# One weight pool for a whole encoder program, with reordered block products and convolution taps that are spread over the next unit

## The chip, the cores and the metric

The kernel runs on one core of a Trainium2 chip. The metric is the time of one execution on the device, in microseconds (us). The engines are PE (TensorE: matrix products), DVE (VectorE), ACT (ScalarE), POOL (GpSimd) and SP (SyncE), whose queue issues nearly all DMAs here. PE accumulates into PSUM banks, which the other engines read; everything else lies in SBUF, 128 partitions wide.

## The reference

One step of a four-part encoder trunk with model width D = 1024 on T = 1152 columns (1024 tokens of a prompt and 8 x 16 tokens of samples). Every part is normalised ahead and added to the stream x:

```
x += attention(rms_norm(x)) @ w_attn_out      # w_attn_in: 1024 -> 3072; 8 band heads, 4 differential heads
x += (silu(h @ wg) * (h @ wu)) @ wd           # h = rms_norm(x), width 2816, twice in all
gb, gc, u = split(rms_norm(x) @ w_conv_in, 3) # 1024 -> 3072
x += (gb * conv3(gc * u)) @ w_conv_out        # three taps along the tokens, one weight per channel
x += (silu(h @ wg) * (h @ wu)) @ wd
y = rms_norm(x)
```

The attention also returns keys and values, the convolution its last two inputs. All of it is float32.

## The kernel before

x lies transposed, as eight tiles of 128 channels by T columns. A float32 product is made of three: each operand is split into a high part, which ACT casts, and a low part, the rest, which DVE subtracts, and PE adds high x high, low x high and high x low (`mm3`, L164 to L166; `pairs`, L1170 to L1172; `unit`, L1033 to L1035).

**Weights.** A piece of 128x512 float32 (256 KB) is loaded by `raw` (tile r, L858) and split by `part` into h (ACT, L868) and l (DVE, L869); RAWS = 5 raw and PARTS = 5 split pieces are in flight. These belong to the pool "w2", which is opened when the attention has closed its own pool. The attention's blocks use another pool, "w1", through `weights`: pieces of 128x1024 (512 KB; tiles wr, wh, wl; L152 to L156), two of each.

**Stages.** The first norm and the attention take up to 645 us of the profiled execution. While the attention's heads are worked off on ACT, DVE and POOL, PE is kept busy with blocks of the in- and out-projection. The last heads' columns of the out-projection (weights in_w_aol) are done by `pairs`, which also serves the three wide products down, conv-out and down: j over 4 pairs of output tiles, six accumulations of 384 columns each; with j = 0 the first inputs k < nk - 1 (here three of four) of all six are done ahead of the last one. Then follow the gates of the first FFN (717 to 1205 us), its down product, the convolution's in-product (1486 to 1796 us), its out-product, and the second FFN, whose down product `down_last` ends the program together with the final norm.

**Units.** Gates and the convolution's in-product are done in units by a seven-product scheme in place of eight (Winograd's form of Strassen's algorithm). A unit has products n = 0 to 6, each in two column halves s of 12 matmuls of 128x288. ORDER names for each the left operand (a sum of weight quarters, made by DVE additions, L990), the right operand (sums of activations, tb11h, tt3h and so on) and the PSUM zone. Behind each half `self.tick()` counts down the pieces of work in `self.late`, so there are 14 ticks in a unit. With product a11, ACT copies the zone to u (L1048) and DVE adds zone b into g (L1049); later DVE adds follow (L1052 to L1065, L1022), POOL multiplies by the norm's factor rb (L1062). With a11 third, the next product, a12, goes into the zone that a11's copy reads.

**The convolution.** A group j has three units: two make the gated inputs xi of channel tiles f, the third the output gate. When a unit of the first kind ends, `end` writes xi and makes the three taps at once: POOL the last one (L1133), DVE the two others (L1136, L1137), POOL the product with rb (L1138).

**The first norm.** Each tile x is split into hh (ACT for even m, POOL for odd m, L196, L198) and hl (DVE, L199); squares on ACT (L207), their sums on POOL for m <= 2, else on DVE (L215); then PE column sums, the root on DVE, diagonals on ACT and POOL (L275, L277), and a spread by PE (L285).

**The order.** A scheduler places the instructions of each engine by priority. Each engine and the SP queue then run their own list in order, and wait where an operand or a buffer isn't ready.

Of the kernel before, what the change touches and what calls it, by code (L numbers as in the profile page):

```python
# [19 lines left out]
P = 128  # L20
D = 1024
# [15 lines left out]
NY = 11  # L37
# [5 lines left out]
NT = 17  # L43
# [56 lines left out]
class K:  # L100
# [45 lines left out]
    def weights(self, src):  # L146

        nc = self.nc
        self.n += 1
        n = self.n  # L150
        raw = self.wp.tile([P, 8, P], F32, tag="wr", name=f"wr_{n}", bufs=2)
        nc.sync.dma_start(raw, src)  # L152
        hi = self.wp.tile([P, 8, P], F32R, tag="wh", name=f"wh_{n}", bufs=self.wbufs)
        lo = self.wp.tile([P, 8, P], F32R, tag="wl", name=f"wl_{n}", bufs=self.wbufs)
        nc.scalar.copy(hi, raw)
        nc.vector.tensor_tensor(lo, raw, hi.bitcast(F32), ALU.subtract)  # L156
        return hi, lo
# [21 lines left out]
    def product(self, ps, w, h, c, step=None):  # L179
        self.mm3(ps, [(w[0][:, k, :], w[1][:, k, :], h[k][0][:, c], h[k][1][:, c]) for k in range(KT)], step)  # L180


    def begin_norm(self, gi, htile, pp, tag, tmp=None, early=False):
        return {"gi": gi, "h": [None] * KT, "rb": [None] * NB, "acc": [None] * NB, "new": htile, "pp": pp, "tag": tag, "tmp": tmp or self.small, "early": early}

    def norm_tile(self, st, m, b, xb):
# [3 lines left out]
        if st["new"] is not None:  # L190
            if st["h"][m] is None:
                st["h"][m] = (st["new"]("hh"), st["new"]("hl"))
            hi, lo = st["h"][m]
            gs = self.g[:, st["gi"], m:m + 1]
            if st["early"] and m % 2:
                nc.gpsimd.tensor_scalar(hi[:, c], xb, gs, 1.0, ALU.mult, ALU.mult)  # L196
            else:
                nc.scalar.activation(hi[:, c], xb, AF.Copy, scale=gs)  # L198
            nc.vector.scalar_tensor_tensor(lo[:, c], xb, gs, hi[:, c].bitcast(F32), ALU.mult, ALU.subtract)  # L199
# [3 lines left out]
    def norm_sum(self, st, m, b, xb):  # L203
        nc = self.nc
        tp = st["tmp"]
# [6 lines left out]
        else:  # L212
            acc = tp("ssq")
            eng = nc.vector if (st["early"] and m > 2) or (st["new"] is None and (m % 2 or m > 5)) else nc.gpsimd
            eng.tensor_tensor(acc, st["acc"][b], sq, ALU.add)  # L215
# [12 lines left out]
    def norm_end(self, st, b):  # L228

        tp = st["tmp"]  # L230
        ps = self.sums(st["pp"], st["tag"], st["acc"][b])
        r = self.rstd(ps[:, :3], D, *[self.tmp(t, (P, 3)) for t in "vty"])
# [11 lines left out]
    def sums(self, pp, tag, sq):  # L244

        ps = self.psum(pp, tag)
        for j in range(3):
# [15 lines left out]
    def diagonals(self, r, tp):  # L263

        nc = self.nc
        parts = self.tmp("rp", (P, 2, 3), F32R)
# [3 lines left out]
        for p in range(2):  # L270
            dg = tp("diag", F32R)
            for j in range(3):
# [8 lines left out]
    def spread(self, pp, tag, dg):  # L281

        ps = self.psum(pp, tag)
# [5 lines left out]
    def accumulate(self, pp, x, y, wsrc, step=None, banks="g"):  # L289
# [4 lines left out]
        for mg in range(KT // per):  # L294
            w = self.weights(wsrc[mg])
            for m in range(mg * per, (mg + 1) * per):
                for b in range(NB):
                    mm = m % per
                    ps = self.psum(pp, banks[(m * NB + b) % len(banks)], (P, 512))[:, :BLK]
                    self.mm3(ps, [(w[0][:, mm * nk + k, :], w[1][:, mm * nk + k, :], y[k][0][:, cut[b]], y[k][1][:, cut[b]]) for k in range(nk)], step)  # L300
# [392 lines left out]
    def subln(self, pp, h):  # L693

        nc = self.nc
        for b in range(NB):
# [7 lines left out]
            r = self.rstd(ps[:, :3], 2 * HD, *[self.tmp(t, (P, 3)) for t in "vty"])  # L704
# [6 lines left out]
    def attention(self, c):  # L711
# [11 lines left out]
        self.wp = pool(right, "w1", side="right")  # L723
        self.wbufs = 2
# [10 lines left out]
        st = self.begin_norm(0, new, pp, "t", self.early, early=True)  # L735
# [107 lines left out]
    def small(self, name, dt=F32):  # L843

        n = {"sq": 4, "ssq": 4, "rb": 3, "diag": 2}[name]
        at = {"sq": 0, "ssq": 4, "rb": 8, "diag": 12}[name] + self.turn.get(name, 0) % n
        self.turn[name] = self.turn.get(name, 0) + 1
        t = self.bits[at // 3][:, at % 3 * BLK:(at % 3 + 1) * BLK]
# [132 lines left out]
    ORDER = (("s2", "t2", "b"), ("s1", "t1", "c"), ("a11", "b11", "a"), ("a12", "b21", "a"), ("s3", "t3", "b"), ("a22", "t4", "b"), ("s4", "b22", "c"))  # L981

    def left_sides(self, w1, w2):
# [12 lines left out]
        split = {"s1": self.part(s1)}  # L996
        s2 = add(s3, a22)
        split["s2"] = self.part(s2)
        split["a11"] = self.part(a11)
# [9 lines left out]
    def unit(self, pp, st, weights, by, end, last=False):  # L1009
# [26 lines left out]

        if first:
            for n in range(3):
                for s in range(2):
                    products(n, s, range(2 if n == 2 else 3))  # L1040
        for n, (wn, p, zn) in enumerate(order):
            for s in range(2):
                products(n, s, range(4) if not first or n > 2 else range(2 if n == 2 else 3, 4))
                ps = zone[zn, s]
                self.tick()
                if n == 2:
# [25 lines left out]
            if n + PARTS < len(order):  # L1072
                ahead = order[n + PARTS][0]
# [29 lines left out]
    def conv(self, pp, st):  # L1103
# [4 lines left out]
        for j in range(KT // 2):  # L1108
            cv = {}
            for f in (2 * j, 2 * j + 1):  # L1110
# [7 lines left out]
                def end(s, g, u, xp=xp, xs=xs, f=f, cv=cv):  # L1118
# [14 lines left out]
                    nc.gpsimd.tensor_scalar(v[:, :SEQ], xp[:, 2:], tap[2], 1.0, ALU.mult, ALU.mult)  # L1133
                    nc.gpsimd.tensor_scalar(vs, xs[:, :, 2:], tap[2], 1.0, ALU.mult, ALU.mult)
                    for t in (1, 0):
                        nc.vector.scalar_tensor_tensor(v[:, :SEQ], xp[:, t:t + SEQ], tap[t], v[:, :SEQ], ALU.mult, ALU.add)  # L1136
                        nc.vector.scalar_tensor_tensor(vs, xs[:, :, t:t + DS], tap[t], vs, ALU.mult, ALU.add)  # L1137
                    nc.gpsimd.tensor_tensor(v, v, st["rb"], ALU.mult)  # L1138
                    cv[f] = v
# [87 lines left out]
    def down_last(self, pp, x, wsrc, chunks):  # L1227
# [14 lines left out]
        self.bits = [self.take("bits")[0] for _ in range(5)]  # L1242
        self.turn = {}
        st = self.begin_norm(4, None, pp, "n")

        def final(b, q, rb):
            for m in (5, 0, 6, 1, 7, 2, 3, 4):
                xb = x[m][:, b * BLK:(b + 1) * BLK]
                if m > 4:
# [3 lines left out]
                nc.sync.dma_start(o["yT"][m][:, b * BLK:(b + 1) * BLK], xb)  # L1253

        st["then"] = final
        for b in range(NB):
            c = slice(b * BLK, (b + 1) * BLK)
            for m in range(KT):
                ps = self.psum(pp, "g", (P, 512))[:, :BLK]
# [4 lines left out]
    def run(self):  # L1264
# [4 lines left out]
        self.xd = self.dp.tile([KT, P, T], F32, name="xd")  # L1269
        x, y = self.attention(c)  # L1270
        with ExitStack() as c:
            pool = lambda name, **kw: c.enter_context(tc.tile_pool(name=name, bufs=1, side="right", reuse_waits="tile", **kw))
            self.wp = pool("w2")
# [133 lines left out]
```

## Time and profile before

| | |
|---|---|
| time, median of 3 runs | 2694.86 us (2690.82 to 2698.37) |
| the profiled execution's own time | 2701.08 us |
| its span, first to last instruction | 2699.2 us |
| mean granted TensorE clock in it | 0.983 |
| PE busy | 2609.2 us, 97% |
| DVE, ACT, POOL busy | 64%, 35%, 22% |
| down, 1250 to 1500 us | PE busy all the time, clock 1.00 |

PE is the engine that sets the time, so its idle time and the stretches with a lower clock are what can be gained without changing the products. The clock column of the profile gives the mean over the stretch; the two levels behind it are 2.4 GHz (1.00) and 1.2 GHz (0.50).

### The profile page before, as it was taken

To read this page: it belongs to the slowest core of one execution; us is meant where nothing else is said; L and a number is where in the kernel's file an instruction comes from. 1 tells how busy PE (TensorE), PEld (TensorE's weight loads), DVE (VectorE), ACT (ScalarE), POOL (GpSimd) and SP (SyncE) were. 2 spreads that over 40 slices of the span, in tenths; PEclk is the share of its full clock that TensorE was granted. 3 is DMA by queue.
4 is the path that set the end of the run, shared out by engine and by line. 5 is a ranking of instruction groups with operands and counts; after the bars stand their busy time and mean duration, and the time that the engine had idled before them with its cause. 6 is when DMAs were issued, how large, how long until landed. Compare 5 with 4: busy or idle time off the path is not lost. (4 is left out here: it accounts for less than half of the span.)

```text
span 2699.2 us, 45160 instructions
## 1 busy us (share of the span) xinstructions
PE 2609.2 (97%) x17440; PEld 2568.3 (95%) x17440; DVE 1715.0 (64%) x3498; ACT 935.1 (35%) x1761; POOL 581.2 (22%) x651
## 2 busy tenths in 40 slices
PE   7999999998999999999999999999999999999997
PEld 6899999988999999999999999999999999999997
DVE  7667766676966666665327877776766666673325
ACT  5555444453532222232104322224422222231114
POOL 6434233320022222220000322320122222210002
PEclk9999999999999999999999999999999999999999
DMA  5654565561022222244212122252322222262211
GB/s 193 186 172 153 169 186 175 173 213 59 32 89 78 77 75 74 76 130 147 69 44 89 49 79 75 62 178 81 117 93 74 74 77 77 76 207 81 66 40 71
DMA packets 179542, 285.71 MB, mean 106 GB/s; under 512 B 38528, under 2 KB 108032, under 8 KB 179328
## 3 DMA queue, kind: packets, MB, share of 16 engines
q1 hardware_dynamic: 179328, 282.84, 33.4%
q8 instruction: 137, 2.24, 0.3%
q14 instruction: 77, 0.63, 0.1%
HBM read 206.67 MB, written 76.10 MB: 105 GB/s over the span
## 5 line engine op out<-in xcount | busy, mean ns | idle before, releaser
L868 ACT CAST h<-r 128x512 fp32r<-128x512 f32 x496 | 305.8, 618 | 960.1 <-PE ps_g L1034 421.6
L869 DVE TENSOR_TENSOR l<-r,h 128x512 fp32r<-128x512 f32 x496 | 359.2, 726 | 127.0 <-ACT h L868 111.8
L1170 PE MATMUL ps_g<-yh,h 128*128 128x384 f32 x1152 | 387.6, 336 | 0.0
L1172 PE MATMUL ps_g<-yh,l 128*128 128x384 f32 x1152 | 387.5, 336 | 0.0
L1171 PE MATMUL ps_g<-yl,h 128*128 128x384 f32 x1152 | 386.7, 336 | 0.0
L1062 POOL TENSOR_TENSOR u<-u,rb 128x576 f32<-128x576 f32 x98 | 158.2, 1634 | 743.2 <-DVE u L1022 725.9
L1183 DVE TENSOR_TENSOR x<-ps_g,x 128x384 f32<-128x384 f32 x240 | 129.4, 552 | 235.3 <-PE ps_g L1172 234.8
L1170 PEld LDWEIGHTS ps_g<-yh,h 128*128 128x128 f32 x1152 | 216.7, 188 | 0.4 <-DVE x L1183 0.2
L1171 PEld LDWEIGHTS ps_g<-yl,h 128*128 128x128 f32 x1152 | 216.5, 188 | 0.0
L1172 PEld LDWEIGHTS ps_g<-yh,l 128*128 128x128 f32 x1152 | 216.4, 188 | 0.0
L164 PE MATMUL ps_g<-hh,wh 128*128 128x384 f32 x544 | 194.4, 358 | 8.9 <-ACT hh L198 6.8
L165 PE MATMUL ps_g<-hl,wh 128*128 128x384 f32 x544 | 186.8, 343 | 1.5 <-DVE hl L199 1.4
L166 PE MATMUL ps_g<-hh,wl 128*128 128x384 f32 x544 | 186.1, 342 | 0.8 <-DVE wl L156 0.8
L990 DVE TENSOR_TENSOR r<-r,r 128x512 f32<-128x512 f32 x224 | 170.8, 762 | 24.8 <-DMA r<-in_w_gu 12.5
L1097 DVE TENSOR_TENSOR g<-g,u 128x576 f32<-128x576 f32 x88 | 66.5, 758 | 148.7 <-ACT g L1096 148.7
L1033 PE MATMUL ps_g<-tb21h,h 128*128 128x288 f32 x448 | 137.4, 307 | 22.2 <-ACT u L1048 22.2
L1033 PE MATMUL ps_g<-tt4h,h 128*128 128x288 f32 x448 | 134.5, 300 | 7.6 <-DVE u L1057 7.6
L1033 PE MATMUL ps_g<-tt3h,h 128*128 128x288 f32 x448 | 135.1, 302 | 2.3 <-DVE g L1049 2.3
L1033 PE MATMUL ps_g<-tb22h,h 128*128 128x288 f32 x448 | 132.9, 297 | 4.5 <-DVE u L1022 4.5
L1035 PE MATMUL ps_g<-tb21h,l 128*128 128x288 f32 x448 | 136.4, 305 | 0.0
L1034 PE MATMUL ps_g<-tb21l,h 128*128 128x288 f32 x448 | 136.1, 304 | 0.0
L1034 PE MATMUL ps_g<-tt3l,h 128*128 128x288 f32 x448 | 134.2, 300 | 0.0
(274 smaller groups left out, 7379.7 us busy)
## 6 DMA issues: line engine op xcount, KB each, us to landing
r<-in_w_gu SPq DMA_DIRECT2D x176, 256.0 KB, 2.7
y<-yd SPq DMA_DIRECT2D x52, 576.0 KB, 4.7
yd<-g SPq DMA_DIRECT2D x96, 288.0 KB, 2.5
r<-in_w_down SPq DMA_DIRECT2D x88, 256.0 KB, 2.7
wr<-in_w_in SPq DMA_DIRECT2D x24, 512.0 KB, 4.4
r<-in_w_cin SPq DMA_DIRECT2D x48, 256.0 KB, 2.7
xd<-x SPq DMA_DIRECT2D x16, 576.0 KB, 2.8
x<-xd SPq DMA_DIRECT2D x16, 576.0 KB, 5.6
```

The source lines that it names most:

```text
L164: nc.tensor.matmul(ps, wh, xh, start=(j == 0), stop=False)
L165: nc.tensor.matmul(ps, wh, xl, start=False, stop=False)
L166: nc.tensor.matmul(ps, wl, xh, start=False, stop=(j == n - 1))
L868: self.nc.scalar.copy(hi, raw)
L869: self.nc.vector.tensor_tensor(lo, raw, hi.bitcast(F32), ALU.subtract)
L990: nc.vector.tensor_tensor(t, x_, y, ALU.add)
L1033: nc.tensor.matmul(ps, w[0][:, k, :], hi, start=(new and k == 0), stop=False, skip_group_check=True)
L1034: nc.tensor.matmul(ps, w[0][:, k, :], lo, start=False, stop=False, skip_group_check=True)
L1062: nc.gpsimd.tensor_tensor(zu[s], zu[s], self.cols(by()[1], s), ALU.mult)
L1170: nc.tensor.matmul(ps, w[q][0][:, e, :], ys[k][0][0][:, c], start=(k == 0), stop=False, skip_group_check=True)
L1171: nc.tensor.matmul(ps, w[q][0][:, e, :], ys[k][1][0][:, c], start=False, stop=False, skip_group_check=True)
L1172: nc.tensor.matmul(ps, w[q][1][:, e, :], ys[k][0][0][:, c], start=False, stop=(k == nk - 1), skip_group_check=True)
```

## The change

- One pool "w" is opened ahead of the attention and stays to the end. `weights` now takes two pieces of 128x512 from it by `raw` and `part`, so the attention shares the five raw and five split pieces with all that follows.
- ORDER has a11 second and s1 third; the pieces are split in that order. The first unit behind a norm keeps the products' old order (seq = 0, 2, 1, 3, ...).
- The taps are entered in `late` and come 1, 2, 4 and 6 ticks into the next unit. The product with rb is DVE's now.
- In the first norm all hh are ACT's and all sums of squares DVE's, as in the last norm.
- `down_last` cuts the columns at 512 and 896, so the last block has 256 columns; the sharing of the final products between POOL and DVE follows the blocks.
- Two buffer counts differ by one (NY, NT).

```diff
-NY = 11
+NY = 10
...
     def weights(self, src):
 
-        nc = self.nc
-        self.n += 1
-        n = self.n
-        raw = self.wp.tile([P, 8, P], F32, tag="wr", name=f"wr_{n}", bufs=2)
-        nc.sync.dma_start(raw, src)
-        hi = self.wp.tile([P, 8, P], F32R, tag="wh", name=f"wh_{n}", bufs=self.wbufs)
-        lo = self.wp.tile([P, 8, P], F32R, tag="wl", name=f"wl_{n}", bufs=self.wbufs)
-        nc.scalar.copy(hi, raw)
-        nc.vector.tensor_tensor(lo, raw, hi.bitcast(F32), ALU.subtract)
-        return hi, lo
+        parts = [self.part(self.raw(src[:, 4 * q:4 * q + 4, :])) for q in range(2)]
+        return [(hi[:, k, :], lo[:, k, :]) for hi, lo in parts for k in range(4)]
...
-            if st["early"] and m % 2:
-                nc.gpsimd.tensor_scalar(hi[:, c], xb, gs, 1.0, ALU.mult, ALU.mult)
-            else:
-                nc.scalar.activation(hi[:, c], xb, AF.Copy, scale=gs)
+            nc.scalar.activation(hi[:, c], xb, AF.Copy, scale=gs)
...
-            eng = nc.vector if (st["early"] and m > 2) or (st["new"] is None and (m % 2 or m > 5)) else nc.gpsimd
-            eng.tensor_tensor(acc, st["acc"][b], sq, ALU.add)
+            nc.vector.tensor_tensor(acc, st["acc"][b], sq, ALU.add)
...
-        self.wp = pool(right, "w1", side="right")
-        self.wbufs = 2
...
-    ORDER = (("s2", "t2", "b"), ("s1", "t1", "c"), ("a11", "b11", "a"), ("a12", "b21", "a"), ("s3", "t3", "b"), ("a22", "t4", "b"), ("s4", "b22", "c"))
+    ORDER = (("s2", "t2", "b"), ("a11", "b11", "a"), ("s1", "t1", "c"), ("a12", "b21", "a"), ("s3", "t3", "b"), ("a22", "t4", "b"), ("s4", "b22", "c"))
...
-        split = {"s1": self.part(s1)}
         s2 = add(s3, a22)
-        split["s2"] = self.part(s2)
-        split["a11"] = self.part(a11)
+        split = {"s2": self.part(s2), "a11": self.part(a11), "s1": self.part(s1)}
...
+        seq = list(range(7))
         if first:
-            for n in range(3):
+            seq = [0, 2, 1, 3, 4, 5, 6]
+            for n in seq[:3]:
                 for s in range(2):
-                    products(n, s, range(2 if n == 2 else 3))
-        for n, (wn, p, zn) in enumerate(order):
+                    products(n, s, range(2 if n == 1 else 3))
+        for n in seq:
+            wn, p, zn = order[n]
             for s in range(2):
-                products(n, s, range(4) if not first or n > 2 else range(2 if n == 2 else 3, 4))
+                products(n, s, range(4) if not first or n > 2 else range(2 if n == 1 else 3, 4))
                 ps = zone[zn, s]
                 self.tick()
-                if n == 2:
+                if n == 1:
                     g, u = zg[s], zu[s] = self.wide("zg", "g"), self.wide("zu", "u")
                     nc.scalar.copy(u[:, 0], ps)
...
-                    nc.gpsimd.tensor_scalar(v[:, :SEQ], xp[:, 2:], tap[2], 1.0, ALU.mult, ALU.mult)
-                    nc.gpsimd.tensor_scalar(vs, xs[:, :, 2:], tap[2], 1.0, ALU.mult, ALU.mult)
-                    for t in (1, 0):
+                    cv[f] = v
+
+                    def last_tap():
+                        nc.gpsimd.tensor_scalar(v[:, :SEQ], xp[:, 2:], tap[2], 1.0, ALU.mult, ALU.mult)
+                        nc.gpsimd.tensor_scalar(vs, xs[:, :, 2:], tap[2], 1.0, ALU.mult, ALU.mult)
+
+                    def tap_of(t):
                         nc.vector.scalar_tensor_tensor(v[:, :SEQ], xp[:, t:t + SEQ], tap[t], v[:, :SEQ], ALU.mult, ALU.add)
                         nc.vector.scalar_tensor_tensor(vs, xs[:, :, t:t + DS], tap[t], vs, ALU.mult, ALU.add)
-                    nc.gpsimd.tensor_tensor(v, v, st["rb"], ALU.mult)
-                    cv[f] = v
+
+                    self.late += [[1, last_tap], [2, lambda: tap_of(1)], [4, lambda: tap_of(0)],
+                                  [6, lambda: nc.vector.tensor_tensor(v, v, st["rb"], ALU.mult)]]
...
-        self.bits = [self.take("bits")[0] for _ in range(5)]
+        self.bits = [self.take("bits")[0] for _ in range(7)]
+        cut = (0, 512, 896, T)
         self.turn = {}
-        st = self.begin_norm(4, None, pp, "n")
+        st = self.begin_norm(4, None, pp, "n", {})
 
         def final(b, q, rb):
             for m in (5, 0, 6, 1, 7, 2, 3, 4):
-                xb = x[m][:, b * BLK:(b + 1) * BLK]
-                if m > 4:
+                xb = x[m][:, cut[b]:cut[b + 1]]
+                if m > (-1, 2, 4)[b]:
                     nc.gpsimd.tensor_tensor(xb, xb, rb, ALU.mult)
                 else:
                     nc.vector.tensor_tensor(xb, xb, q, ALU.mult)
-                nc.sync.dma_start(o["yT"][m][:, b * BLK:(b + 1) * BLK], xb)
+                nc.sync.dma_start(o["yT"][m][:, cut[b]:cut[b + 1]], xb)
...
+        self.wp = c.enter_context(tc.tile_pool(name="w", bufs=1, side="right", reuse_waits="tile"))
         x, y = self.attention(c)
         with ExitStack() as c:
             pool = lambda name, **kw: c.enter_context(tc.tile_pool(name=name, bufs=1, side="right", reuse_waits="tile", **kw))
-            self.wp = pool("w2")
```

Lines of the changed kernel stand some 10 to 15 lower: L868 is L856 there, L990 is L978, L1048 is L1037, L1136 is L1129.

Where the orders differ, two places are shown. The first is DVE in the convolution, from the taps of the second channel tile on (cv is the tap sum, xi its input, l and r weight pieces, g and u a unit's outputs). Before:

```order
L1136 SCALAR_TENSOR_TENSOR cv_17449<-xi_17167,convw,cv_17449 128x1024
L1137 SCALAR_TENSOR_TENSOR cv_17449<-xi_17167,convw,cv_17449 128x128
L1136 SCALAR_TENSOR_TENSOR cv_17449<-xi_17167,convw,cv_17449 128x1024
L1137 SCALAR_TENSOR_TENSOR cv_17449<-xi_17167,convw,cv_17449 128x128
L869 TENSOR_TENSOR l_17520<-r_17461,h_17519 128x512
L990 TENSOR_TENSOR r_17710<-r_17706,r_17708 128x512
L869 TENSOR_TENSOR l_17550<-r_17483,h_17549 128x512
L990 TENSOR_TENSOR r_17712<-r_17704,r_17706 128x512
L990 TENSOR_TENSOR r_17718<-r_17712,r_17708 128x512
L1049 TENSOR_TENSOR g_17566<-ps_g_17493,u_17567 128x288
L869 TENSOR_TENSOR l_17715<-r_17710,h_17714 128x512
L1049 TENSOR_TENSOR g_17583<-ps_g_17506,u_17584 128x288
```

With the change:

```order
L1129 SCALAR_TENSOR_TENSOR cv_17613<-xi_17331,convw,cv_17613 128x1024
L1130 SCALAR_TENSOR_TENSOR cv_17613<-xi_17331,convw,cv_17613 128x128
L857 TENSOR_TENSOR l_17681<-r_17618,h_17680 128x512
L1129 SCALAR_TENSOR_TENSOR cv_17613<-xi_17331,convw,cv_17613 128x1024
L1038 TENSOR_TENSOR g_17697<-ps_g_17650,u_17698 128x288
L1130 SCALAR_TENSOR_TENSOR cv_17613<-xi_17331,convw,cv_17613 128x128
L978 TENSOR_TENSOR r_17874<-r_17870,r_17872 128x512
L857 TENSOR_TENSOR l_17721<-r_17640,h_17720 128x512
L1038 TENSOR_TENSOR g_17716<-ps_g_17665,u_17717 128x288
L1133 TENSOR_TENSOR cv_17613<-cv_17613,rb_17383 128x1152
L978 TENSOR_TENSOR r_17876<-r_17868,r_17870 128x512
L978 TENSOR_TENSOR r_17878<-r_17876,r_17872 128x512
L1043 TENSOR_TENSOR g_17697<-ps_g_17684,cv_17407 128x288
```

The four tap instructions stood in a row, ahead of all of the next unit's work. Now a weight piece, the additions into g (L1038 there) and a weight sum stand between them, and the product with rb (L1133 there, 128x1152) is behind them as a fifth.

The second place is the SP queue at the end of the attention (o are the heads' outputs, stored to and loaded from DRAM; olo is a head's last part). Before, from the last outputs to the first weights of `pairs`:

```order
L790 DMA o_8497<-o_86 128x384
L570 DMA o_86<-olo_8477 64x512
L790 DMA o_8501<-o_86 128x384
L790 DMA o_8505<-o_86 128x384
L858 DMA r_8533<-in_w_aol 128x512
L858 DMA r_8539<-in_w_aol 128x512
L858 DMA r_8643<-in_w_aol 128x512
L858 DMA r_8649<-in_w_aol 128x512
L858 DMA r_8765<-in_w_aol 128x512
```

With the change:

```order
L778 DMA o_8651<-o_89 128x384
L778 DMA o_8655<-o_89 128x384
L778 DMA o_8659<-o_89 128x384
L846 DMA r_8703<-in_w_aol 128x512
L846 DMA r_8807<-in_w_aol 128x512
L846 DMA r_8813<-in_w_aol 128x512
L846 DMA r_8929<-in_w_aol 128x512
L680 DMA o_89<-os_8277 128x64
L846 DMA r_8935<-in_w_aol 128x512
L846 DMA r_9062<-in_w_aol 128x512
L560 DMA o_89<-olo_8391 64x512
```

Six of the eight pieces of in_w_aol show here, ahead of the third last store of olo; the very first stands 48 rows above the first of these. Before, all eight stood behind the last load of o. Behind the rows shown there follow now the eighth piece, a store, a load, two pieces of in_w_gu (the FFN's weights), the last store of olo and the last two loads of o, in this order.

## Rows read from the trace of the kernel before

**Rows 1.** The page's first part: busy time, share of the span, instructions.

```profile
PE 2609.2 (97%) x17440; PEld 2568.3 (95%) x17440; DVE 1715.0 (64%) x3498; ACT 935.1 (35%) x1761; POOL 581.2 (22%) x651
```

**Rows 2.** Waits of PE: waiting line, what it waited for: us, times, longest.

```profile
PE ps_g L1033 <- ACT u L1048: 22.2, 12, 2.2
PE ps_g L1170 <- ACT h L868: 9.3, 1, 9.3
PE ps_g L1033 <- DVE u L1057: 7.6, 4, 3.9
...
PE ps_t L285 <- ACT diag L275: 4.1, 2, 2.4
```

**Rows 3.** Windows: PE, PEld, DVE, ACT, POOL busy (instructions), clock, DMA share, GB/s.

```profile
100.00:640.00 540.00, 529.19 (x3446) 504.18 (x3445) 380.97 (x1173) 273.96 (x641) 164.25 (x274) 0.99 0.55 170
1500.00:1800.00 300.00, 275.74 (x1951) 272.55 (x1951) 220.66 (x358) 68.83 (x124) 101.35 (x85) 0.95 0.28 78
650.00:660.00 10.00, 5.40 (x21) 5.18 (x22) 4.44 (x7) 4.12 (x7) 0.00 (x0) 0.58 0.86 265
1600.00:1610.00 10.00, 7.82 (x48) 7.58 (x48) 8.69 (x12) 1.54 (x3) 2.39 (x1) 0.83 0.13 27
1300.00:1350.00 50.00, 50.00 (x289) 50.00 (x288) 20.38 (x28) 12.04 (x15) 0.00 (x0) 1.00 0.26 78
```

**Rows 4.** Waits of PE between 1500 and 1800 us.

```profile
PE ps_g L1033 <- ACT u L1048: 14.5, 7, 2.2
```

**Rows 5.** Timeline of one stall: start, duration, engine, line [idle before <- releaser].

```profile
1599.35 3.05 POOL L1138 TENSOR_TENSOR cv<-cv,rb 128x1152 f32<-128x1152 f32 x1 [2.84 <-DVE cv L1137]
1599.90 3.04 DVE L990 TENSOR_TENSOR r<-r,r 128x512 f32<-128x512 f32 x1
1603.05 0.62 ACT L868 CAST h<-r 128x512 fp32r<-128x512 f32 x1 [3.91 <-DVE r L990]
1603.58 0.39 ACT L1048 COPY u<-ps_g 128x288 f32<-128x288 f32 x1
1603.58 0.69 DVE L990 TENSOR_TENSOR r<-r,r 128x512 f32<-128x512 f32 x1
1604.02 0.61 PE L1033 MATMUL ps_g<-tb21h,h 128*128 128x288 f32 x1 [2.18 <-ACT u L1048]
```

**Rows 6.** Timeline of the change from attention to `pairs`, SP, DVE and PE.

```profile
646.64 0.45 SPq L570 DMA_DIRECT2D o<-olo  x1
649.82 6.45 SPq L858 DMA_DIRECT2D r<-in_w_aol  x7
651.86 1.16 DVE L792 TENSOR_TENSOR ol<-o,oh 128x384 fp32r<-128x384 f32 x2 [5.24 <-ACT oh L791]
654.60 0.69 PE L1170 MATMUL ps_g<-oh,h 128*128 128x384 f32 x1 [9.32 <-ACT h L868]
```

**Rows 7.** Groups by line and shape: count, busy us, mean ns, idle before.

```profile
L949 DVE TENSOR_TENSOR ssq<-ssq,sq 128x1152 f32<-128x1152 f32 x21 | 28.3, 1350 | 0.5 <-ACT sq L948 0.5
L1138 POOL TENSOR_TENSOR cv<-cv,rb 128x1152 f32<-128x1152 f32 x8 | 27.5, 3433 | 22.8 <-DVE cv L1137 22.8
L196 POOL TENSOR_SCALAR hh<-x,gains 128x384 fp32r<-128x384 f32 x12 | 13.4, 1126 | 10.5 <-DMA x<-in_xT 10.5
L199 DVE SCALAR_TENSOR_TENSOR hl<-x,gains,hh 128x384 fp32r<-128x384 f32 x24 | 19.3, 817 | 0.5 <-POOL hh L196 0.5
L378 DVE SCALAR_TENSOR_TENSOR zl<-z,zh 128x384 fp32r<-128x384 f32 x48 | 27.1, 564 | 33.0 <-POOL zh L377 28.1 <-DMA k<-s 2.2 <-DMA on<-ob 1.8
L155 ACT CAST wh<-wr 128x1024 fp32r<-128x1024 f32 x28 | 29.4, 1048 | 26.2 <-PE ps_g L165 21.5 <-DMA wr<-in_w_in 3.2 <-PE ps_v L165 1.4
```

**Rows 8.** Timeline, PE's waits at the convolution's end and in the second FFN's first gates.

```profile
1793.33 0.61 PE L1033 MATMUL ps_g<-tb22h,h 128*128 128x288 f32 x1 [4.48 <-DVE u L1022]
1943.22 0.61 PE L1033 MATMUL ps_g<-tt4h,h 128*128 128x288 f32 x1 [3.92 <-DVE u L1057]
```

**Rows 9.** Timeline of the program's end, SP.

```profile
2692.78 3.78 SPq L1253 DMA_DIRECT2D out_yT<-x  x8
```

## What the change was expected to do

> **What bounds the kernel now.** I read the page's busy table first: PE is busy 97% of the span [rows 1], so the kernel can't be made faster by speeding up another engine as such, only by removing what PE waits for. Then the table of PE's waits [rows 2]: few kinds of waits hold nearly all of it, and the reader should see two things: one kind comes twelve times at about 2 us, another once at 9.3 us. Then windows [rows 3], for where these lie and for the clock. In the down product PE is busy for all of 50 us at clock 1.00, with 289 matmuls of 384 columns: 50/289 = 0.173 us each, which is the full-speed price that I use below. In the convolution's 300 us PE is busy for 275.7, so 24.3 are idle, and the mean clock is 0.95: at the lower of the two levels for a tenth of the time, which costs up to (1 - 0.95) x 300 = 15 us more. The whole stage can thus give back about 39 us and no more. The window 1600 to 1610 shows the two together: 2.18 us idle, and then a clock of 0.83 over these 10 us, that is (1 - 0.83) x 10 = 1.7 us. So I count a 2-us wait as nearly 4.
>
> Last the timeline of one such wait [rows 5], read from the bottom: PE's product a12 waits 2.18 us for ACT's copy of a11 (L1048). The copy takes 0.39 us and wasn't itself late for PE's data; it stands behind a weight cast (L868) in ACT's list, which waited 3.91 us for DVE's weight sum L990. And that sum took 3.04 us where the next one takes 0.69. What is special in it is what POOL does just then: the 3.05 us product cv x rb (L1138) covers nearly the same time.
>
> **The change, part by part.** I make the sum against the profiled execution's 2701.1 us (6.2 above the median shown) and scale at the end.
>
> *One pool.* Before, the eight in_w_aol loads are issued from 649.82 on, behind everything else of the attention; PE resumes at 654.60 after 9.32 us [rows 6]. With the change five of these loads need no finished attention, by the SP order shown, so the first product of `pairs` has its weights. What is late next is the last head: its store was issued at 646.64 and its low part was finished by 651.86 + 1.16 = 653.0 [rows 6]. Before it is needed, `pairs` can do 3 of 4 inputs for six accumulations, 6 x 3 x 3 = 54 matmuls, 54 x 0.173 = 9.3 us; from 645.3 on that lasts till 654.6, past the head's 653.0. So the whole 9.3 goes. The clock: between 650 and 660 PE had 21 matmuls in 5.4 us [rows 3], at full price 3.6 us, so 1.8 more. I take -11; bounds: -6 if the head comes some 5 us late behind the weights that now stand ahead of its stores, and -13 if PE's drop ahead of 645 shrinks too. The cost: 28 loads become 56. Two casts of 128x512 instead of one of 128x1024 add ACT and DVE time, but these are at 274 and 381 of 540 us in the attention [rows 3], and apart from the switch itself no wait in [rows 2] is for a weight's cast. Free unless the queue order turns against it (rival 3).
>
> *The order and the taps.* With a11 second, product s1's two halves (2 x 12 matmuls) lie between a11 and a12, so ACT's copy has that much more time before a12 writes its zone. By its columns a matmul of 288 costs 288/384 of 0.173, 0.13 us; 24 x 0.13 = 3.1 us more slack against waits of at most 2.2 [rows 2]. The 14.5 us of these waits in the convolution [rows 4] should go, at 7 x 1.7 = 12 us of clock beside them. Independent of that, the port clash goes: cv x rb moves to DVE, where a two-input operation on the same 128x1152 takes 1.35 us as against 3.43 on POOL [rows 7]. DVE gets 8 x 1.35 = 10.8 us more and loses 2.3 us of stretching per clash; it is busy 221 of 300 us there [rows 3], so it has room on average, though it is nearly full in the units that also split y tiles. The remaining 24.3 - 14.5 = 9.8 idle us are DVE's: 4.48 at the end behind late y tiles [rows 8], the rest additions that come late. I take half of those with half of their clock. Sum: full would be -39; I take -27, with -14 (only the copies' direct waits) and -39 as bounds.
>
> The Trainium skill's page "GPSIMD Engine Reference", section "Specifications", says that GpSimd shares its SBUF interfaces with VectorE and that VectorE instructions with two SBUF inputs contend. The trace agrees, with 3.04 against 0.69 us for the same addition [rows 5]; by it the products u x rb, which stay on POOL, would go on stretching DVE, and rival 1 would be what happens.
>
> *The same order in the FFNs.* 22.2 - 14.5 = 7.7 us of copy waits, 5 in number, lie outside the convolution. Those in a first unit behind a norm, where the order is kept, stay; I take three of the five as gone, about 5 us, with 1.7 us of clock each: up to -10. The 3.9 us wait for L1057 [rows 8] comes from a y tile's split ahead of it, and the order leaves that alone. I take -6, bounds 0 and -10.
>
> *First norm.* POOL's hh take 1.13 us [rows 7] and go to ACT; hl, which took 0.82 us on average under POOL, should take nearer to 0.56, like the same form elsewhere: 24 x 0.25 = 6 us less DVE, against a few more sums. PE waits 4.1 us for diagonals there [rows 2], and also starts at a low clock after them. I take -6; bounds -9 and 0, since ACT's casts of weights now share its list with twice as many hh.
>
> *Last blocks.* The eight final outputs still need eight DMA issues, 3.78/8 = 0.47 us each [rows 9], which sets the end; narrower columns shorten the products ahead of it by some tenths each, and the 256-column block covers less of the second block's norm. I take 0, bounds -2 and +3. NY, NT: 0.
>
> Sum: -11 - 27 - 6 - 6 + 0 = -50, so 2651 for a profiled execution; times 2694.86/2701.08 that is 2645 us.
>
> **The rivals.** *1. The convolution is DVE's to lose.* Taps and product now stand between the additions that PE waits for: the product, 1.35 us by [rows 7], directly ahead of the two weight sums and of L1043. If DVE comes late there, the copy's waits are replaced by waits for L1043 and L1046. For it: DVE's share of 74% is a mean, and POOL products that stay still stretch it. Against: the stretched operation and its 3-us product are gone, and the taps no longer come in one block. It would halve the convolution's gain: 2645 + 13 = 2658, and the table of waits would show L1046 or L1008 with 8 us or more in that stage.
>
> *2. The switch stays.* Two in_w_gu loads, whose buffers come free by DVE's splits, stand ahead of the last head's store. If they hold it by more than 1.6 us (54 matmuls to 654.6 against 653.0), PE waits in the 55th matmul instead of the first; at worst the gain of 11 is gone: 2656. For it: queue order. Against: the pieces that they wait for are loaded several us earlier.
>
> *3. Slower: the shared pieces stall the attention.* The ACT casts of weights waited 26.2 us before, 28 times, so 0.94 each, most of it for PE to free a buffer [rows 7]; ACT works in order, and softmax work stands behind them. With 56 casts the wait may be had 56 times. To eat the 50 us, each of the 56 would have to pass 50/56 = 0.9 us on to PE: then 2695, no gain, and beyond it slower. At 1.1 us each it is 2706. Against: before, these 26.2 us passed at most 540 - 529.2 = 10.8 us to PE [rows 3], and five pieces let the loads run further ahead than two pairs did.
>
> *4. No change that can be told:* the convolution's and the FFNs' waits return in full before other products (a22 behind s3, for DVE), and the switch stays. Of the 50 only the first norm's 6 are left: 2701 - 6, scaled 2689. For it: L1057's waits, which the order doesn't touch [rows 2]. Against: none of these is more than a third of the copy's.
>
> **How the numbers follow.** The forecast 0.62, rival 1 0.16, rival 2 0.12, rival 3 0.04, rival 4 0.06. A change of 0.3% (8 us) is about what can be told. Rivals 1 and 2 are still faster, so faster has 0.90, same 0.06, slower 0.04. The range: low, all 39 of the convolution and the better bounds of the starts, 2645 - 12 - 4 - 3 - 2 = 2624; high, half of the convolution lost (+13), the switch's worse bound (+5), both starts at nothing (+12) is 2675, and I put it at 2676, which leaves out little more than rivals 3 and 4. Within the forecast alone it is 2632 to 2658.
>
> **What would show it.** Right: no wait of PE for in_w_aol near 650 us; the copy's waits at under 5 us in all; clock of the convolution above 0.97 and PE idle under 10 us in it; weight sums L978 all near 0.7 us there; the first norm's diagonal waits under 3 us. Wrong: waits of PE of the same total under other names (L1043, L1046, L1008) in the convolution; new waits for softmax or weight casts between 100 and 640 us; a gap at the change to `pairs` that only moved; DVE over 85% in the convolution.

## The result and the profile after

The changed kernel takes 2667.63 us (median of 4 runs, 2665.76 to 2672.99) beside 2696.51 us for the kernel before on the same chips (4 runs, 2690.82 to 2698.37). The ratio is 0.990, with a 95% interval of 0.988 to 0.992: 28.9 us faster, clear of noise and inside the stated range, but little more than half of the 50 that were forecast. The profiled execution took 2665.76 us.

The page's first row and the whole program's largest waits of PE, of the changed kernel, as in [rows 1] and [rows 2]:

```profile
PE 2595.4 (97%) x17440; PEld 2553.2 (96%) x17440; DVE 1700.7 (64%) x3539; ACT 941.1 (35%) x1801; POOL 541.2 (20%) x626
```

```profile
PE ps_g L1019 <- DVE u L1046: 23.6, 14, 9.6
PE ps_g L156 <- ACT hh L187: 6.0, 1, 6.0
...
PE ps_t L275 <- POOL diag L267: 3.4, 2, 2.1
PE ps_t L275 <- ACT diag L265: 1.6, 1, 1.6
...
PE ps_g L1019 <- ACT u L1037: 1.4, 2, 1.1
```

Two rows have all but gone: the wait for in_w_aol (9.3 us, now not in the table), and that for ACT's copy of a11 (L1048 before, L1037 now; 22.2 us, now 1.4). But a new one leads: 14 waits for L1046, an addition of DVE that was L1057 with 7.6 us before. The two lines together stood at 29.8 us before and stand at 25.0 now: by their sum, what changed is mostly the name.

To see what each stage gave, I take the start of each stage's first matmul from the timelines and subtract. Stage lengths in us:

| | to out-product | out-product | first gates | down | convolution | conv-out | second gates | down, end | span |
|---|---|---|---|---|---|---|---|---|---|
| before | 654.6 | 52.4 | 503.2 | 276.0 | 310.1 | 101.3 | 507.0 | 294.5 | 2699.2 |
| changed | 642.9 | 50.4 | 505.0 | 276.0 | 293.9 | 100.3 | 498.9 | 296.4 | 2663.8 |

The attention and the change to `pairs` gave 11.7 + 2.0, the convolution 16.2, the second gates 8.1; the first gates and the end cost 1.8 and 1.9. Among kernels below that share the attention's code, its length varies from 642.9 to 647.0 (the changed kernel's is the shortest), so single differences of 3 us there say nothing. The first gates vary from 503.5 to 509.0 in the same way, so their 1.8 says nothing either.

The convolution of the kernel before as a window (columns as in [rows 3]):

```profile
1486.27:1796.38 310.11, 285.85 (x2042) 282.66 (x2042) 230.77 (x375) 77.68 (x140) 98.73 (x84) 0.95 0.28 78
```

Windows of the changed kernel: the convolution, and the 20 us around the change to `pairs`, which now have no gap:

```profile
1474.00:1768.00 294.00, 276.77 (x2042) 274.46 (x2041) 220.28 (x386) 77.84 (x139) 75.25 (x78) 0.98 0.30 82
640.00:650.00 10.00, 10.00 (x62) 10.00 (x61) 3.39 (x9) 2.81 (x7) 0.53 (x1) 1.00 0.25 79
650.00:660.00 10.00, 10.00 (x59) 10.00 (x58) 8.06 (x14) 6.46 (x10) 0.00 (x0) 1.00 0.09 28
```

In the convolution 294 - 276.8 = 17.2 us are still idle (24.3 before), and the clock is 0.98 (0.95). So idle time fell by some 7 us, and PE's busy time for the same 2042 matmuls by some 9: more than half of the stage's 16.2 us is clock. Its waits, in one row:

```profile
PE ps_g L1019 <- DVE u L1046: 17.2, 9, 9.6
```

One of the nine is 9.57 us, in the last unit; the other eight are 0.6 to 1.8 us, at most one in a unit. The timeline of the long one:

```profile
1739.52 0.55 SPq L1118 DMA_DIRECT2D out_cs<-xi  x1
1740.18 0.60 SPq L1211 DMA_DIRECT2D x<-xd  x1
...
1748.13 0.32 SPq L1211 DMA_DIRECT2D x<-xd  x1
1748.54 0.38 SPq L1147 DMA_DIRECT2D y<-yd  x1
1756.88 1.15 ACT L856 CAST yh<-y 128x1152 fp32r<-128x1152 f32 x1 [12.42 <-DMA y<-yd]
1758.06 1.36 DVE L857 TENSOR_TENSOR yl<-y,yh 128x1152 fp32r<-128x1152 f32 x1 [7.58 <-ACT yh L856]
1759.34 0.45 DVE L1046 TENSOR_TENSOR u<-ps_g,u 128x288 f32<-128x288 f32 x1
1759.84 0.61 PE L1019 MATMUL ps_g<-tt4h,h 128*128 128x288 f32 x1 [9.57 <-DVE u L1046]
```

From the bottom: PE waits for L1046, which stands in DVE's list behind the low part of a y tile for the out-product, which waits for ACT's high part, which waits for the y load (tile y, from the DRAM tensor yd), issued at 1748.54. That load stood in SP's queue behind a load of x, issued at 1748.13. What held the load of x is in SP's own waits of that stretch:

```profile
SPq L1211 <- DMA out_cs<-xi: 3.9, 1, 3.9
```

out_cs is the store of the convolution's last inputs, issued at 1739.52 out of xi's tile.

### The profile page after: what moved, and what is told of

It is laid out like the page before. It is cut to its first block, busy times and chain, and to the rows that moved or that the text cites. A ratio compares the mean times of both kernels' runs of the same rounds, so it can differ in the third digit from the quotient of the medians.

```text
span 2663.8 us, 45287 instructions
## 1 busy us (share of the span) xinstructions
PE 2595.4 (97%) x17440; PEld 2553.2 (96%) x17440; DVE 1700.7 (64%) x3539; ACT 941.1 (35%) x1801; POOL 541.2 (20%) x626
## 5 line engine op out<-in xcount | busy, mean ns | idle before, releaser
L856 ACT CAST h<-r 128x512 fp32r<-128x512 f32 x552 | 338.2, 617 | 995.8 <-PE ps_g L1020 496.5
L857 DVE TENSOR_TENSOR l<-r,h 128x512 fp32r<-128x512 f32 x552 | 398.5, 724 | 131.9 <-ACT h L856 117.7
L156 PE MATMUL ps_g<-hh,h 128*128 128x384 f32 x544 | 196.8, 362 | 10.8 <-ACT hh L187 6.0
L157 PE MATMUL ps_g<-hl,h 128*128 128x384 f32 x544 | 188.3, 346 | 0.2 <-DVE hl L188 0.2
L158 PE MATMUL ps_g<-hh,l 128*128 128x384 f32 x544 | 186.9, 344 | 0.0
L978 DVE TENSOR_TENSOR r<-r,r 128x512 f32<-128x512 f32 x224 | 154.5, 690 | 32.7 <-DMA r<-in_w_gu 15.1
L1085 ACT ACTIVATE g<-g 128x576 f32<-128x576 f32 x88 | 60.2, 685 | 208.3 <-POOL g L1056 207.5
L1020 PE MATMUL ps_g<-tt4l,h 128*128 128x288 f32 x448 | 133.8, 299 | 0.0
L1020 PE MATMUL ps_g<-tb11l,h 128*128 128x288 f32 x448 | 132.1, 295 | 1.6 <-DVE tb11l L886 1.6
L1021 PE MATMUL ps_g<-tt4h,l 128*128 128x288 f32 x448 | 133.6, 298 | 0.0
```

The costliest lines, as they stand in the source:

```text
L156: nc.tensor.matmul(ps, wh, xh, start=(j == 0), stop=False)
L157: nc.tensor.matmul(ps, wh, xl, start=False, stop=False)
L158: nc.tensor.matmul(ps, wl, xh, start=False, stop=(j == n - 1))
L856: self.nc.scalar.copy(hi, raw)
L857: self.nc.vector.tensor_tensor(lo, raw, hi.bitcast(F32), ALU.subtract)
L1020: nc.tensor.matmul(ps, w[0][:, k, :], lo, start=False, stop=False, skip_group_check=True)
```

## The experiments

Two theories stood against each other for the convolution. **Theory O**: the order freed ACT's copy, as the forecast has it. **Theory C**: the copy was late only because POOL's product stretched DVE's weight sums, and taking that product off POOL is what helped. All ratios are to the kernel before, with 95% intervals.

**e1: the changed kernel with the old order.** The pieces are split in the old order too.

```diff
-    ORDER = (("s2", "t2", "b"), ("a11", "b11", "a"), ("s1", "t1", "c"), ...
+    ORDER = (("s2", "t2", "b"), ("s1", "t1", "c"), ("a11", "b11", "a"), ...
```

> The changed kernel with the old order of products (s1 ahead of a11); pool, taps, norm and cuts as changed. Convolution stage: 310.3 us before, 294.1 changed. Theory O (the order is what freed ACT's copy of a11): the copy's waits come back, 10 us or more in the convolution, the stage takes 304 to 310, in all 2678 to 2684 us. Theory C (the port clash was what made ACT late, and it is gone with the product on DVE): the copy's waits stay under 4 us, the stage takes 292 to 297, in all 2666 to 2671.

2666.9 us, 0.9889 (0.9864 to 0.9914): the same time as the changed kernel. The convolution takes 279.9 us, shorter than either theory had it. Its waits of PE, and those in the out-product behind it:

```profile
PE ps_g L1165 <- DVE u L1010: 2.5, 1, 2.5
PE ps_g L1021 <- ACT u L1038: 2.4, 3, 1.0
PE ps_g L1165 <- DVE g L1055: 1.6, 2, 1.1
PE ps_g L1021 <- DVE u L1047: 1.5, 2, 1.1
PE ps_g L1021 <- DVE g L1039: 1.1, 1, 1.1
```

The copy's waits don't come back (2.4 us with the old order, 14.5 before [rows 4]), and the stage has its full clock:

```profile
1479.00:1759.00 280.00, 274.79 (x2042) 271.31 (x2041) 214.25 (x380) 74.99 (x135) 70.18 (x75) 1.00 0.29 80
```

Theory O falls. Beside the kernel before, the convolution of e1 is 30.2 us shorter, without the new order; which part of that is the product's engine and which the spread taps, with the old order, wasn't tried. The 14 us that it is shorter than in the changed kernel are given back by the out-product, 107.2 (100.3 changed), the second gates, 503.6 (498.9), and 4 us of the attention's variation.

**e8: the kernel before with the new order alone.** The same edit the other way, on the kernel before.

> The kernel before with only the new order of products. Theory O: nearly all that the convolution and the second gates gained comes with it: convolution 294 to 298, second gates near 499 (507.2 before), in all 2670 to 2675. Theory C: the late weight sums now reach PE by way of L1057 instead of the copy, convolution 304 to 310, in all 2686 to 2695.

2690.76 us, 0.9979 (0.9967 to 0.9992): about 6 us. The convolution takes 306.6 us, and all of its waits have the new name (L1058 is L1057 of the kernel before):

```profile
PE ps_g L1031 <- DVE u L1058: 25.2, 9, 9.1
```

The order moves the wait and hardly shortens it. The second gates, 499.2, are as short as in the changed kernel, while e1 with the old order has 503.6: 5 to 8 us of the second gates' gain are the order's.

**e2 and e3: the taps in one block as before; the product with rb back on POOL.** In e2, the whole old end of `end`; in e3 one word:

```diff
-  [6, lambda: nc.vector.tensor_tensor(v, v, st["rb"], ALU.mult)]]
+  [6, lambda: nc.gpsimd.tensor_tensor(v, v, st["rb"], ALU.mult)]]
```

> The changed kernel with all three taps and the product with rb (on POOL) issued when the unit ends, as before. Theory O: with the new order the clash costs PE little, stage 293 to 298, in all 2666 to 2672. Theory C: weight sums take 3 us again under the product, DVE comes late at L1046, stage 300 to 306, in all 2674 to 2680.

> The changed kernel with only the product cv x rb back on POOL, still at the sixth tick. If the remaining waits for L1046 come from DVE having too much ahead of it (1.34 us of product), they shrink: stage 288 to 292, in all 2662 to 2666. If the clash costs DVE more than the product does (3.0 instead of 0.7 us for a weight sum just there), they grow: stage 297 to 303, in all 2671 to 2677.

e2 takes 2682.23 us, 0.9942 (0.9924 to 0.9961); e3 2680.4 us, 0.9944 (0.9921 to 0.9966). The convolution takes 308.7 and 306.4; times and stages lie 2 to 4 us beyond the slower of the two cases expected. So the product's engine alone is worth 12.8 us (2680.4 against 2667.6), and spreading the taps beside it about 2, which isn't told from noise. The first rows are one place in e3, POOL and DVE; the last two are the wait in e3 and the weight sums of all units (count, busy us, mean ns):

```profile
1591.59 0.68 DVE L978 TENSOR_TENSOR r<-r,r 128x512 f32<-128x512 f32 x1
1591.75 3.64 POOL L1133 TENSOR_TENSOR cv<-cv,rb 128x1152 f32<-128x1152 f32 x1 [3.84 <-DVE cv L1130]
1593.16 3.50 DVE L978 TENSOR_TENSOR r<-r,r 128x512 f32<-128x512 f32 x2
...
PE ps_g L1019 <- DVE u L1046: 24.2, 9, 9.0
...
L978 DVE TENSOR_TENSOR r<-r,r 128x512 f32<-128x512 f32 x224 | 169.3, 756 | 35.8 <-DMA r<-in_w_gu 16.5 <-DMA r<-in_w_cin 12.9 <-DVE l L857 3.2
```

Two weight sums, the first begun under the product, take 3.50 us, where one takes 0.68 ahead of it. In the changed kernel no sum in the convolution takes more than 0.83 us, and their mean over the program is lower:

```profile
L978 DVE TENSOR_TENSOR r<-r,r 128x512 f32<-128x512 f32 x224 | 154.5, 690 | 32.7 <-DMA r<-in_w_gu 15.1 <-DMA r<-in_w_cin 11.3 <-DVE l L857 4.2
```

So Theory C stands: with the product on POOL the sums beside it take some 2.8 us again, and PE's waits for L1046 are 24.2 us instead of 17.2.

**e12: without the product.** The line of e3 is left out, and with it the norm's factor in the taps' sum.

> The changed kernel without the product cv x rb in the convolution: this leaves the norm's factor out of the taps' sum, so the output of the convolution is not the reference's, and only the time is read. It takes 1.34 us from DVE's list in each of eight units. If PE's waits for L1046 there come from what stands ahead of it in DVE's list, those of 0.6 to 1.8 us (8 in number, 7.7 us together) fall to under 3 us together, convolution 284 to 289, in all 2656 to 2662. If they come from late loads of weights (DVE waits 11.3 us for these in the changed kernel), they stay above 6 us, convolution 292 to 295, in all 2665 to 2670. The 9 us wait at the convolution's end stays either way.

2659.48 us, 0.9868 (0.9852 to 0.9885), convolution 289.2 us:

```profile
PE ps_g L1019 <- DVE u L1046: 13.5, 5, 9.9
```

Beside the long wait (9.9 us) four remain, together 3.6 (7.7 in the changed kernel; the first case had them under 3), while DVE's own waits for weight loads are as they were (11.1 us). So about half of the small waits are the product's place in DVE's list, just ahead of L1046; the rest isn't explained by it.

**e4: a small copy of the convolution's last inputs.** The store of xi holds xi's tile, so a later load into that tile waits for it.

```diff
-                    nc.sync.dma_start(o["cp"][f], xp[:, SEQ:SEQ + 2])
-                    nc.sync.dma_start(o["cs"][f], xs[:, :, DS:DS + 2])
+                    last = u[:, 0, :2 + 2 * DB]
+                    nc.gpsimd.tensor_scalar(last[:, :2], xp[:, SEQ:SEQ + 2], 1.0, 1.0, ALU.mult, ALU.mult)
...
+                    nc.sync.dma_start(o["cp"][f], last[:, :2])
```

> The changed kernel, but the convolution's last inputs go to the output from a small copy that POOL makes in a used part of u, so that the tile xi is free as soon as the taps have read it. The 9.57 us wait of PE at the convolution's end: if a load of x, held by the store of xi, holds up the y load behind it in SP's queue, the load of x goes out some 4 us earlier, the wait falls to 5 to 6.5, convolution 288 to 291 (293.9 changed), in all 2661 to 2665. If the y load waits for its own buffer or for the DMA engines beside the x loads, the wait stays at 9 to 10 and the time at 2665 to 2671.

2665.02 us, 0.9886 (0.9871 to 0.9901). The long wait fell to 5.83 us, as the theory of the held x load has it:

```profile
PE ps_g L1019 <- DVE u L1046: 16.4, 9, 5.8
...
1762.05 0.61 PE L1019 MATMUL ps_g<-tt4h,h 128*128 128x288 f32 x1 [5.83 <-DVE u L1046]
```

But the eight others grew from 7.7 to 16.4 - 5.8 = 10.6 us, while POOL's two copies now stand beside the last tap, on which DVE's taps wait (8.0 us of such waits in the changed kernel, some 11 here). The convolution stays at 294.1 us. Half of the expectation failed: the cause was right, the remedy costs as much.

**e5 and e10: pools and pieces.** e5 gives the changed kernel two weight pools again; e10 gives the kernel before only the attention's weights in 128x512 pieces (and NY = 10, NT = 18 for the room).

```diff
-        self.wp = c.enter_context(tc.tile_pool(name="w", ...))
+        self.wp = pool(right, "w1", side="right")
...
+            self.wp = pool("w2")
```

> The changed kernel with a weight pool of its own for the attention (same pieces, same counts), closed before the second one opens, as before. If the pool was the cause of the stall at the change from attention to pairs, PE waits some 9 us for the first weights again, the stages up to the first gates take 702 to 706 us (693.3 changed), in all 2676 to 2681. If the last head is the limit and the smaller pieces did the rest, PE waits at most 3 us there, in all 2666 to 2671.

> The kernel before with the attention's weights in pieces of 128x512 through raw and part (and the two buffer counts that make room for them), still in a pool of its own that closes first. If the piece size was what removed the stall, PE waits under 2 us at the change to pairs (9.3 before), the stages up to the first gates take 694 to 698 us (707.0 before), in all 2684 to 2688. If the one pool matters, the stall stays at 7 us or more and the time at 2692 to 2698.

e5 takes 2668.7 us, 0.9902 (0.9887 to 0.9916): not told from the changed kernel. e10 takes 2683.31 us, 0.9954 (0.9938 to 0.9971), 13.7 us less than the kernel before. PE's wait at the change to `pairs`, in e5 and then in e10:

```profile
PE ps_g L1165 <- ACT h L857: 1.2, 1, 1.2
```

```profile
PE ps_g L1162 <- ACT h L860: 1.2, 1, 1.2
```

1.2 us in both, where it was 9.3 [rows 2]. One pool isn't needed for this (e5), and the pieces alone are enough (e10): in e10 the first three loads of in_w_aol stand ahead of the last store of olo in SP's queue, while in the kernel before the first of them goes out at 649.82, behind that store [rows 6].

```profile
637.25 1.45 SPq L850 DMA_DIRECT2D r<-in_w_aol  x3
648.33 0.45 SPq L562 DMA_DIRECT2D o<-olo  x1
```

Why is not shown. That each new piece lies on one old piece of its own size is my reading of the code; the pieces are also half as large, and five of them are in flight instead of two, and these weren't told apart.

Not all of e10's 13.7 us lies there. Its stages up to the first gates take 698.8 us, 8.3 less than before and a little beyond the 694 to 698 expected. Its convolution, with the code of the kernel before, takes 304.7 us, 5.4 less at about the same idle time and a higher clock:

```profile
1479.06:1783.76 304.70, 279.90 (x2042) 276.74 (x2042) 229.69 (x375) 77.67 (x140) 98.41 (x84) 0.97 0.28 79
```

So some 5 of the 16.2 us that the convolution gave can belong to the one profiled execution of the kernel before.

**e6 and e7: POOL in the first norm again; the old cuts.**

> The changed kernel with POOL's share of the first norm as before (hh of odd tiles, first sums of squares). By the forecast it should be 6 us slower: PE's waits in the first 100 us grow, attention ends near 649 (642.9 changed), in all 2672 to 2675. By the traces of before and changed alone, which end the attention's blocks only about 2 us apart beside the stall, it is 1 to 3 us slower, in all 2666 to 2672.

> The changed kernel with the last stage cut at 384 and 768 as before, and POOL with the last three of eight final products of each block. If the new cuts are what made the end 2 us longer (69.8 from the last pair of down to the end, 67.8 before), the end takes 67.5 to 68.5 and all 2663 to 2668; if the sums on DVE did, it stays at 69.5 or more and 2665 to 2671.

e6 takes 2671.49 us, 0.9912 (0.9895 to 0.9928), e7 2665.69 us, 0.9888 (0.9874 to 0.9903). Neither is told from the changed kernel. For e6, the first 60 us are the better measure: PE gets 225 matmuls done in the changed kernel, 214 in e6, 208 before; at about 0.17 us that is 2 to 3 us. In the changed kernel three of e6's five diagonal waits are left (5.0 of 6.7 us), but PE then waits 2.63 us for DVE's product of a projection with the cosines (z) instead. In e7 the end, behind the last product of `pairs`, takes 69.2 us, 0.8 less than in the changed kernel and between the two cases expected.

**e9 and e11: versions.** e9 uses the old order in the convolution and the new one in the FFNs. e11 adds e4's copy and e7's cuts.

```diff
+            self.old = True
             st = self.begin_sides(2, pp, (i["w_cin"][8], i["w_cin"][16]), True)
...
+            self.old = False
             st = self.begin_sides(3, pp, gu(1)(0), True)
```

> The changed kernel with the old order of products in the convolution alone and the new one in both FFNs. With e1's convolution (279.9) and out-product (107.2) and the changed kernel's second gates (498.9) the sum is 4 to 5 us under e1: 2661 to 2664 us. If the out-product or the gates give back what the convolution gains (2.5 us of wait and a low clock at the out-product's start are such), 2665 to 2669.

> As the mixed order, with the small copy for the convolution's last inputs and the old cuts of the last blocks. If x loads held by the store of xi are what delays the y tiles at the convolution's end, the out-product falls from 107 to 100 to 103 us, in all 2652 to 2658. If not, it stays at 105 or more, in all 2659 to 2664.

e9 takes 2661.78 us, 0.9872 (0.9846 to 0.9899), as the first case expected; convolution 280.0, conv-out 107.9, second gates 499.4. e11 takes 2659.57 us, 0.9858 (0.9828 to 0.9888): conv-out 104.2, between its two cases, and convolution 283.1, so here too the copy gives in one stage and takes in the other. Both are faster than the kernel before by 1.3 to 1.4%; their distance from the changed kernel, 6 and 8 us, lies at the edge of what these runs tell.

## Why the prediction was right and where it was off

The total lies in the stated range, but above the 2632 to 2658 that the prediction gave for the forecast alone: in the convolution rival 1 came, and most other terms were somewhat smaller than forecast. Of the signs named, four came as for "right": no wait for in_w_aol, the copy's waits at 1.4 us, the convolution's clock at 0.98 and its weight sums at most 0.83 us. But PE is idle for 17.2 us there, where under 10 were asked for, in waits for L1046, a sign of "wrong".

- *What bounds the kernel* held: PE's waits and the clock behind them make up the gain, and every stage without waits kept its time (down: 276.0 in all kernels but for 0.3).
- *One pool, -11*: the size was about right, 9.3 us of wait and 2.0 in the out-product by the changed kernel's trace, 8.3 by e10's. The cause was not the pool: e10 has this gain without the common pool, e5 keeps it with two. The number came out because the new pieces were part of the same change, not because the step named was the one that worked.
- *The order and the taps, -27*: this is the mis-sized term; it measured -16.2. The step that failed is "with a11 second ... ACT's copy has that much more time", with the sentence that the 14.5 us "should go". The copy's waits went, but DVE's waits grew from 9.8 to 17.2 us, now for L1046: the order gives the copy slack and takes no work from DVE, whose list was the late one. Rival 1 named this line and this place; its price (13 us less) was near the 11 that were missing. e8 shows the order worth little alone, e1 that it costs the convolution 14 us beside the other changes. The -27 itself comes out of its parts only with half of all the clock (14.5 + 4.9 + 7.5); with the 12 us of clock named beside the copy's waits they add up to some 33, still farther off. What did work is the product on DVE, which the forecast had as a second, "independent" gain without a size of its own: 12.8 us by e3. DVE pays for it in its list: without any product (e12) the stage is 4.7 us shorter.
- *The half of DVE's waits*: the forecast took half of these 9.8 us as gone, 4.48 of them at the end. The end's wait grew to 9.57. With the new order alone (e8) it is 9.1 us already, and with the old order beside the other changes (e1) it is gone from the convolution and reaches the out-product as 2.5 us: the y tile's low part stands ahead of L1046 with the new order, and PE needs that addition earlier than the one it waited for before.
- *FFN gates, -6*: the second gates gave 8.1, the first took 1.8, sum -6.3. e8 and e1 show 5 to 8 of the second gates' as the order's; the first gates' part lies within their variation.
- *First norm, -6*: the forecast was too high; it is 2 to 3 us by matmuls done, 3.9 by e6's times within their noise. The diagonal waits were 5.0 us, not under 3: they went from 4.1 for ACT's and 1.9 for POOL's to 1.6 and 3.4, so POOL's own diagonals took over as the last.
- *Last blocks, 0*: +1.9 in the trace, inside the bounds of -2 and +3. e7 puts some 0.8 of it on the cuts (e11, with the same old cuts, ends in 68.5 us, 1.5 less than the changed kernel); the rest stays open, the sums on DVE being the main other change there.

The sum by stages is -35.4 us between the two profiled executions: of the 50, the order and the taps lack 10.8, pool and first norm together 3.3. Between medians it is -28.9; the profiled execution of before lies 4.6 above its median and that of the changed kernel 1.9 below.

## What to carry to other kernels

When a wait's chain runs through three engines, price the operation at its far end (here a weight sum that took 3.04 instead of 0.69 us) before giving slack to the nearest one: slack at the wrong link only renames the wait. An order that costs nothing on the engine it is made for has to be read on the in-order list of each engine that serves it. When a change has two parts, here a common pool and smaller pieces, try each by itself before naming the cause: the pieces alone gave what the pool was credited with.

## What the runs showed of the hardware

A VectorE addition with two inputs took 0.68 us for 128x512 alone, and up to 3.06 us in the kernel before, while GpSimd multiplied two tensors of 128x1152: in [rows 5] it ended 0.5 us behind that product. In the changed kernel no weight sum of the convolution took more than 0.83 us. The Trainium skill's "GPSIMD Engine Reference" ("Specifications") says that GpSimd shares its SBUF interfaces with VectorE, and that VectorE instructions with two SBUF inputs contend. The trace agrees, and it shows how much of it is a matter of place: GpSimd's products u x rb (1.63 us) and its last tap (1.19 us) stayed on GpSimd, and VectorE instructions went on being stretched beside the products: some splits, the longest 1.92 us at 1524.41, and seven of the sixteen products for xi (L1109), which took 1.66 to 1.68 us, where the others took 0.45:

```profile
1570.70 1.67 DVE L1109 TENSOR_TENSOR xi<-g,u 128x288 f32<-128x288 f32 x1 [0.94 <-POOL u L1051]
...
1572.90 0.45 DVE L1109 TENSOR_TENSOR xi<-g,u 128x288 f32<-128x288 f32 x1
```

No run took u x rb off GpSimd, so what it still costs PE is open. The clash with cv x rb was worth a factor of 4 to 5 on one addition and 13 us on the program (e3).

The store of the convolution's last inputs, 128x8x2 numbers in rows of two, was issued at 1739.52, and the load into its tile went out at 1748.13: some 8 us for 8 KB. Out of e4's small copy, where the numbers of a partition lie side by side, the same store took 2.7 us from issue to landing (median of eight), against 7.1 in the changed kernel.

In the convolution of the kernel before, the clock over the 10 us behind each of six waits of 2.0 to 2.2 us was 0.83 (the wait in the window of 1600 to 1610 in [rows 3] is one of them). In the changed kernel it was 1.00 behind seven waits of 0.6 to 1.2 us and 0.83 behind one of 1.83, and e1 kept 1.00 over its convolution with 5.2 us idle. This is no rule: in the second gates of the changed kernel a wait of 2.05 us (at 1912.19) left the clock at 1.00, and at the start of its first gates it was 0.83 behind waits of 1.1 us.
